# Split-weight tiles 64 bytes longer each, so that their offsets modulo 512 all differ

## The chip, the cores and the metric

The kernel runs on one core of a Trainium2 chip. The metric is the device time of one execution in microseconds (us), the median of three runs. A profile of one more execution gives the busy times of the engines: TensorE with its matmuls (PE) and its weight loads (PEld), VectorE (DVE), ScalarE (ACT), GpSimd (POOL) and the queue of SyncE (SP).

## What is computed

Two transformer blocks, one after the other, over 256 tokens of width 2048, in float32. The first mixes a gated linear attention and a sparse attention and ends with a feed-forward layer of width 5632; the second is an attention layer with modulation and a pooling layer. Cut to what matters here, it is a chain of matrix products with large weights:

```
proj = rms_norm(x, g) @ w_in                       # 2048 x 5672
h    = x + concat([gla_out, nsa_out]) @ w_out
x    = h + (silu(m @ w_gate) * (m @ w_up)) @ w_down   # 5632 wide
...
proj = h @ ev_w_in;   x = x + gate * _rmsnorm(y @ ev_w_out, post_g)
proj = h @ od_w_in;   x = x + gate * _rmsnorm(y @ od_w_out, post_g)
```

## The kernel before

**A product in three passes.** Every large product is made of float32r matmuls. Both sides are split into a high part and a remainder (hi = the value cast to float32r, lo = value - hi), and hi*hi, lo*hi and hi*lo are added up in PSUM. A job (class Job) is one panel of 512 weight columns. It goes through its K dimension in chunks of two tiles of 128 rows (per = 2), and `run` handles the chunks of all jobs in one list. For chunk i it issues the load of the weights of chunk i+4 into a tile `raw` (line 293, SP queue), splits those of chunk i+2 in `cut` (line 314: ACT casts raw to whi; line 315: DVE subtracts, raw - whi to wlo), and issues the matmuls of chunk i in `part`. raw has 6 buffers in the pool wp; whi and wlo have 3 each in wp. In two short stretches of the second block (the end of each output product) every other group of three chunks takes its whi and wlo from a pool of its own, "lead".

**Plain and turned jobs.** In a plain job the weights move: TensorE loads 128 columns of an activation tile (xh or xl) as the stationary operand, and 512 columns of whi or wlo stream through (lines 360 to 362; a chunk has 2 token halves x 2 tiles of K x 3 = 12 matmuls). In a turned job the activations move: 128 columns of whi or wlo are the stationary operand, and the 256 tokens of xh or xl stream through (lines 350 to 352; 4 x 2 x 3 = 24 matmuls per chunk). Every matmul loads its own stationary operand first.

**Where the activations lie.** The pairs xh, xl ([128, 16, 256] float32r, 16,384 bytes per partition each) are in actA for the first projection, the gate and up products, the context, and both output products of the second block; in actB for the first output product, two of the three down products, and the inputs of the second block's two layers; in the pool ffn for one down product. The inputs of the four small products of the pooling layer, ph and pl, lie in the pool pl2. Plain jobs with actA as the stationary operand have 3,744 matmuls, with actB 2,016, with ffn 384. Turned jobs with actA as the moving operand have 768 (the first projection), with actB 1,536, with ph/pl 192.

**Offsets in a partition.** Pools on the left are stacked in the order cp, xp, wp, actA, sp, actB, modp, lead; those on the right (ffn, pl2 and the pools of the attentions among them) grow down from the top, 229,376. Each tile's size is rounded up to 32 bytes. Adding this up gives, in bytes:

| tiles | start | modulo 512 |
|---|---|---|
| raw, 6 of 4,096 | 40,288 | 352 (o) |
| whi, 3 of 4,096 | 64,864 | o |
| wlo, 3 of 4,096 | 77,152 | o |
| actA: xh, xl | 89,440 and 105,824 | o |
| sp (scratch, 14,528 in all) | 122,208 | |
| actB: xh, xl | 136,736 and 153,120 | 32 (o + 192) |
| lead: whi, wlo | 181,088 | o |
| ffn: xh, xl; pl2: ph, pl | 196,576 and 212,960; 208,864 and 212,960 | 480 (o + 128) |
| the raw tiles of `compress`; its split tiles | 139,680; 157,856 | 416; 160 |

The small products in the attentions have tiles at other offsets: the first attention's values at 160, the second's keys and values at 416. `gla` uses gsumt and lah at 160. The table's last row belongs to line 900, which subtracts as line 315 does.

**The two scratch tiles.** `small(n, tag, bufs)` takes a tile from sp, which stays open to the end. `post_small` (the gates, line 705) uses ge, 48 floats, and `compress` (line 932) uses hs, 64 floats; each has one buffer and is used once.

Of the kernel before, what the change touches and what calls it, by code (L numbers as in the profile page):

```python
# [11 lines left out]
F32 = mybir.dt.float32  # L12
F32R = mybir.dt.float32r
# [6 lines left out]
P = 128  # L20
# [105 lines left out]
def emit(ctx, tc, a, out, dbg=None, stop=None):  # L126
# [8 lines left out]
    def pool(name, side, **kw):  # L135
        return tc.tile_pool(name=name, bufs=1, side=side, **kw)
# [3 lines left out]
    wp = ctx.enter_context(pool("wp", "left"))  # L140
# [6 lines left out]
    def nm(s):  # L147
        cnt[0] += 1
        return f"{s}_{cnt[0]}"
# [12 lines left out]
    def small(n, tag="sm", bufs=4):  # L162
        return sp.tile([P, n], F32, tag=f"{tag}{n}", name=nm(tag), bufs=bufs)
# [14 lines left out]
    def split(src, hi, lo, scale=None):  # L178

        if scale is None:  # L180
            S.copy(hi, src)  # L181
            V.tensor_tensor(lo, src, hi, OP.subtract)  # L182
        else:
            S.activation(hi, src, AF.Copy, scale=scale)
            V.scalar_tensor_tensor(lo, src, scale, hi.bitcast(F32), OP.mult, OP.subtract)
# [55 lines left out]
    def wait(*jobs):  # L241
        while not all(j.task and j.task.done for j in jobs):
            yield
# [22 lines left out]
                    mods.popleft()  # L266

    LOAD, SPLIT = 4, 2
    raws, splits = {}, {}

    def raw_tile():
# [2 lines left out]
    def run(jobs):  # L274
# [22 lines left out]
        def cut(i, eng=V):  # L297
            if i >= len(seq) or i in splits:
                return
            j, c = seq[i]  # L300
            nk, n = len(j.chunks[c]), j.n
            raw = raws.pop(i)
            wpool, bufs = (env["lead"], 3) if env.get("lead") and (i - env["lead0"]) % 6 >= 3 else (wp, 3)
            hi = wpool.tile([P, 2, 512], F32R, tag="whi", name=nm("whi"), bufs=bufs)
            lo = wpool.tile([P, 2, 512], F32R, tag="wlo", name=nm("wlo"), bufs=bufs)
            if j.per != 2:
                hi, lo = (t.rearrange("p k n -> p (k n)")[:, :nk * n].rearrange("p (k n) -> p k n", n=n) for t in (hi, lo))
            splits[i] = (hi, lo)
            if i == 0:
                for k in range(2):  # L310
                    x_split(0, (k,))()
                    split(raw[:, k, :], hi[:, k, :], lo[:, k, :])
                return
            S.copy(hi[:, :nk, :n], raw[:, :nk, :n])  # L314
            eng.tensor_tensor(lo[:, :nk, :n], raw[:, :nk, :n], hi[:, :nk, :n], OP.subtract)  # L315
# [152 lines left out]
    env = {}  # L468
# [77 lines left out]
    def x_split(c, ks=(0, 1)):  # L546
        def f():
            for j in ks:
                k = 2 * c + j
                split(xts[c][:, j, :], nx[0][:, k, :], nx[1][:, k, :], attn_g[:, k:k + 1])  # L550
        return f
# [139 lines left out]
    def post_small(ps):  # L691

        lrT, la, gates = env["lrT"], env["la"], env["gates"]
        V.memset(lrT, 1.0)
        V.tensor_tensor(lrT[:40, :], ps[0][:40, :T], Rrow[:40, :], OP.mult)
        yield
        yield from wait(jk1)
        pt = bank("t")[:, :80].rearrange("p (m n) -> p m n", m=2)
        zs = [bank(t) for t in "os"]
        for m in range(2):  # L700
            TE.transpose(pt[:, m, :], lrT[:40, tok(m)], ident[:40, :40])
        for m in range(2):
            TE.matmul(zs[m], lrT[:, tok(m)], env["w2aug"], start=True, stop=True)
        yield
        ge = small(48, "ge", 1).rearrange("p (m n) -> p m n", m=2)
        S.activation(ge, pt[:, :, 16:], AF.Exp, scale=-1.0)
        az = [tk() for _ in range(2)]
        for m in range(2):
            S.activation(az[m], zs[m], AF.Abs)
            V.tensor_scalar(la[:, m, :], zs[m], 0.0, None, OP.min)  # L710
        V.tensor_scalar(ge, ge, 1.0, None, OP.add)
        V.reciprocal(gates, ge)
        yield
        for m in range(2):
            S.activation(az[m], az[m], AF.Exp, scale=-1.0)
        yield
        for m in range(2):
            S.activation(az[m], az[m], AF.Ln, bias=ones)
        yield
        for m in range(2):  # L720
            V.tensor_tensor(la[:, m, :], la[:, m, :], az[m], OP.subtract)
# [157 lines left out]
    def compress():  # L879

        kgs = env["kgs"]
        env["es_cmp"] = ExitStack()
        cpp = env["cpp"] = env["es_cmp"].enter_context(pool("cmp", "right"))
        raws_, cuts_ = {}, {}
        seq = [(kv, c) for kv in range(2) for c in range(4)]

        def w1_load(i):
            if i < 8:
                kv, c = seq[i]
                t = raws_[i] = cpp.tile([P, 2, 4, P], F32, tag="w1", name=nm("w1"), bufs=2)  # L890
                for h in range(2):
                    r0 = (16 * h + 4 * c) * P
                    Y.dma_start(t[:, h], a[("cmp_k_w1", "cmp_v_w1")[kv]][r0:r0 + 4 * P, :].rearrange("(o d) j -> d o j", d=P))

        def w1_cut(i):
            if i < 8:
                t = raws_.pop(i)
                hi, lo = cuts_[i] = [cpp.tile([P, 2, 4, P], F32R, tag=f"w1{n}", name=nm("w1"), bufs=b) for n, b in (("h", 2), ("l", 1))]
                S.copy(hi, t)
                V.tensor_tensor(lo, t, hi, OP.subtract)  # L900

        w1_load(0)
        w1_load(1)
        w2t = cpp.tile([P, 2, P], F32, name="w2t")
        for kv in range(2):
            G.dma_start(w2t[:, kv, :], a[("cmp_k_w2", "cmp_v_w2")[kv]])
        csel = cpp.tile([68, 60], F32, name="cselt")
        G.dma_start(csel, a["csel"])
        yield
        w1_cut(0)  # L910
        yield from wait(jkcvc)
        U = env["U"]
        hp = bank("o")
        for i, (kv, c) in enumerate(seq):
            hi, lo = cuts_.pop(i)
            o = hp[:, kv * 256:(kv + 1) * 256]
            w1_load(i + 2)
            for j in range(4):
                first = c + j == 0
                TE.matmul(o[:68], U[kv][:, 4 * c + j, :], hi[:, :, j, :], start=first, stop=False, skip_group_check=True)  # L920
            for j in range(4):
                TE.matmul(o[:34], U[kv][:, 4 * c + j, :34], lo[:, :, j, :], start=False, stop=c + j == 6, skip_group_check=True)
            w1_cut(i + 1)
            yield
        seg = cpp.tile([P, 2, 4, P], F32, tag="w1", name=nm("seg"), bufs=2)[:68, :, :2, :]
        S.copy(seg, hp[:68, :].rearrange("p (v a j) -> p v a j", v=2, a=2))
        yield
        hp = bank("o")
        for kv in range(2):
            for k in range(2):  # L930
                TE.matmul(hp[:, 32 * kv:32 * kv + 30], seg[:, kv, k, :], csel[:, 30 * k:30 * k + 30], start=k == 0, stop=k == 1)
        hs = small(64, "hs", 1)
        for kv in range(2):
            S.activation(hs[:, 32 * kv:32 * kv + 30], hp[:, 32 * kv:32 * kv + 30], AF.Silu)
        yield
        op_ = bank("o")
        for kv in range(2):
            for h in range(2):
                c0 = 32 * kv + h * NCMP
                TE.matmul(op_[:NCMP, (2 * kv + h) * P:(2 * kv + h + 1) * P], hs[:, c0:c0 + NCMP], w2t[:, kv, :],  # L940
                          start=True, stop=True)
        yield
        V.tensor_copy(env["vcN"], op_[:NCMP, 256:512].rearrange("p (h d) -> p h d", d=P))
        kc = cpp.tile([P, 2, 4, P], F32, tag="w1", name=nm("kc"), bufs=2)[:, 0, :2, :]
        ss = small(2, "kcs")
        for h in range(2):
            S.activation(kc[:NCMP, h, :], op_[:NCMP, h * P:(h + 1) * P], AF.Square, accum_out=ss[:NCMP, h:h + 1])
        rr = rsqrt_mean(ss[:NCMP], 2, P, "kcr", NCMP)
        yield
        for h in range(2):  # L950
            V.tensor_scalar(kc[:NCMP, h, :], op_[:NCMP, h * P:(h + 1) * P], rr[:NCMP, h:h + 1], None, OP.mult)
        yield
        pt = bank("o")
        for h in range(2):
            TE.transpose(pt[:, h * 16:h * 16 + NCMP], kc[:NCMP, h, :], ident[:NCMP, :NCMP])
        yield
        V.tensor_scalar(env["kcT"], pt[:, :32].rearrange("p (h n) -> p h n", n=16)[:, :, :NCMP], kgs[:, 0:1], None, OP.mult)
        dump("kcT", env["kcT"])
        dump("vcN", env["vcN"])
        env["es_cmp"].close()  # L960
# [986 lines left out]
```

## Time and profile before

| | |
|---|---|
| median of 3 runs | 1950.67 us (1948.8 to 1950.82) |
| the profiled execution | 1954.03 us |
| its span, first to last instruction | 1952.3 us |
| PE busy | 1904.4 us, 98% |
| PEld busy | 1623.0 us, 83% |
| DVE busy | 1422.0 us, 73% |
| ACT busy | 956.8 us, 49% |
| DMA | 443.17 MB, mean 227 GB/s |

Busy times are those of one execution. Matmuls are pipelined: a matmul's record lasts longer than the distance to the start of the next, so the rate is read from the starts.

### The profile page before, as it was taken

How to read it: one execution, taken by the hardware profiler on the slowest of the kernel's cores; microseconds unless marked ns; L12 is line 12 of the kernel's file. 1: busy time of each engine (PE TensorE's matmuls, PEld its weight loads, DVE VectorE, ACT ScalarE, POOL GpSimd, SP SyncE). 2: the span in 40 equal slices, each digit the busy share in tenths (PEclk: the TensorE clock that was granted, in tenths of full speed). 3: DMA queues.
4: the chain of work that ended last, by engine and by line, in shares of the span. 5: the costliest groups of instructions: out<-in, count | busy, mean ns of one | idle time of the engine just before them, and what ended most of it. 6: DMA issues, size and time to landing. Idle time of an engine off the chain costs nothing.

```text
span 1952.3 us, 26733 instructions
## 1 busy us (share of the span) xinstructions
PE 1904.4 (98%) x10070; PEld 1623.0 (83%) x10070; DVE 1422.0 (73%) x1915; ACT 956.8 (49%) x1353; POOL 143.7 (7%) x142
## 2 busy tenths in 40 slices
PE   8999999999999999999999999999999998999998
PEld 8898778888888888888888787877999976999986
DVE  5767987688887888876667776569887777765554
ACT  6655456665444444444445444345556545544443
POOL 1001420000000000000000000012111003200001
PEclk9999999999999999999999999999999999999999
DMA  8675343478888888778987886465666695776544
GB/s 301 183 245 152 109 131 107 168 241 270 263 266 268 261 270 264 264 270 284 334 285 248 307 309 204 145 215 179 191 198 195 243 334 188 249 230 183 181 173 172
DMA packets 212434, 443.17 MB, mean 227 GB/s; under 512 B 18466, under 2 KB 27728, under 8 KB 211664
## 3 DMA queue, kind: packets, MB, share of 16 engines
q1 hardware_dynamic: 211536, 439.41, 68.2%
q0 software_dynamic: 768, 2.05, 0.3%
q8 instruction: 79, 1.29, 0.3%
q14 instruction: 51, 0.42, 0.1%
HBM read 439.29 MB, written 2.11 MB: 226 GB/s over the span
## 4 chain that ended last, share of the span: by engine, by line
PE 83%; DVE 5%; DMA 4%; ACT 4%; POOL 2%; issue 1%; SPq 0%; DVEq 0%; ACTq 0%; POOLq 0%
PE g L362 21%; PE g L360 21%; PE g L361 20%; PE g L350 5%; PE g L352 5%; PE g L351 5%; DVE wlo L315 1%; DMA raw<-in_w_down_dram 1%; ACT whi L314 1%; PE s L196 1%; DMA raw<-in_w_gate_dram 1%; PE o L1555 1%; PE t L196 1%; DMA raw<-in_od_mod_w_dram 1%; POOL E L757 1%
## 5 line engine op out<-in xcount | busy, mean ns | idle before, releaser
L315 DVE TENSOR_TENSOR wlo<-raw,whi 128x1024 fp32r<-128x1024 f32 x592 | 725.9, 1230 | 379.2 <-ACT whi L314 375.8
L314 ACT CAST whi<-raw 128x1024 fp32r<-128x1024 f32 x600 | 628.8, 1050 | 699.0 <-PE g L361 511.8
L360 PE MATMUL g<-whi,xh 128*128 128x512 f32 x2048 | 809.2, 395 | 3.5 <-ACT xh L1357 2.1
L362 PE MATMUL g<-wlo,xh 128*128 128x512 f32 x2048 | 802.4, 392 | 5.5 <-DVE wlo L315 5.5
L361 PE MATMUL g<-whi,xl 128*128 128x512 f32 x2048 | 801.4, 391 | 2.2 <-DVE xl L1362 2.2
L362 PEld LDWEIGHTS g<-wlo,xh 128*128 128x128 f32 x2048 | 385.5, 188 | 92.6 <-DVE wlo L315 9.5
L360 PEld LDWEIGHTS g<-whi,xh 128*128 128x128 f32 x2048 | 385.9, 188 | 85.5 <-ACT xh L1357 3.8
L361 PEld LDWEIGHTS g<-whi,xl 128*128 128x128 f32 x2048 | 385.8, 188 | 84.8 <-DVE xl L1362 4.8
L512 DVE SCALAR_TENSOR_TENSOR raw<-raw,crow 128x1024 f32<-128x1024 f32 x192 | 235.5, 1227 | 18.1 <-DMA raw<-in_od_mod_w_dram 8.8
L350 PE MATMUL g<-xh,whi 128*128 128x256 f32 (+1 forms) x784 | 222.3, 284 | 3.2 <-ACT whi L314 2.6
L352 PE MATMUL g<-xh,wlo 128*128 128x256 f32 (+1 forms) x784 | 220.3, 281 | 0.9 <-DVE wlo L315 0.5
L351 PE MATMUL g<-xl,whi 128*128 128x256 f32 (+1 forms) x784 | 220.0, 281 | 0.0
L350 PEld LDWEIGHTS g<-xh,whi 128*128 128x128 f32 (+1 forms) x784 | 148.1, 189 | 5.1 <-ACT whi L314 2.8
L352 PEld LDWEIGHTS g<-xh,wlo 128*128 128x128 f32 (+1 forms) x784 | 148.3, 189 | 1.7 <-DVE wlo L182 0.9
L351 PEld LDWEIGHTS g<-xl,whi 128*128 128x128 f32 (+1 forms) x784 | 148.3, 189 | 0.5
L512 DVE SCALAR_TENSOR_TENSOR mjk<-raw,crow 128x1024 bf16<-128x1024 f32 x64 | 78.0, 1218 | 2.6 <-ACT crow L501 2.0
L1537 POOL TENSOR_TENSOR P<-P,rc 128x512 f32<-128x512 f32 x32 | 34.2, 1069 | 161.5 <-DVE rc L1536 139.9
L189 POOL TENSOR_SCALAR crt<-rss 128x2 f32<-128x2 f32 x1 | 1.1, 1092 | 495.2 <-DVE rss L1280 495.2
L1529 ACT ACTIVATE P<-s,ngm 128x512 f32<-128x512 f32 x32 | 22.1, 690 | 26.5 <-DVE ngm L1522 13.8
L189 POOL TENSOR_SCALAR rrt<-rs 128x2 f32<-128x2 f32 x2 | 1.3, 642 | 405.2 <-DVE rs L1175 405.2
L196 PE MATMUL s<-ident,P 128*128 128x128 f32 x176 | 26.8, 275 | 1.0 <-DVE ngm L1519 0.6
L181 ACT CAST xh<-s 128x512 fp32r<-128x512 f32 x27 | 15.9, 588 | 22.2 <-PE s L196 22.2
(356 smaller groups left out, 1481.5 us busy)
## 6 DMA issues: line engine op xcount, KB each, us to landing
raw<-in_ev_mod_w_dram SPq DMA_DIRECT2D x96, 512.0 KB, 4.7
raw<-in_od_mod_w_dram SPq DMA_DIRECT2D x96, 512.0 KB, 4.9
raw<-in_w_gate_dram SPq DMA_DIRECT2D x88, 512.0 KB, 4.6
raw<-in_w_up_dram SPq DMA_DIRECT2D x88, 512.0 KB, 4.6
raw<-in_w_down_dram SPq DMA_DIRECT2D x88, 512.0 KB, 5.3
raw<-in_w_in_dram SPq DMA_DIRECT2D x87, 512.0 KB, 3.7
raw<-in_ev_w_in_dram SPq DMA_DIRECT2D x80, 512.0 KB, 4.4
raw<-in_od_w_in_dram SPq DMA_DIRECT2D x64, 512.0 KB, 4.5
```

The source lines that it names most:

```text
L196: TE.transpose(pt[:, j * P:(j + 1) * P], src[:, j * P:(j + 1) * P], ident)
L314: S.copy(hi[:, :nk, :n], raw[:, :nk, :n])
L315: eng.tensor_tensor(lo[:, :nk, :n], raw[:, :nk, :n], hi[:, :nk, :n], OP.subtract)
L350: TE.matmul(o, hi[:, k, ws], xh[:, xk, :], **b, stop=False, skip_group_check=True)
L351: TE.matmul(o, hi[:, k, ws], xl[:, xk, :], start=False, stop=False, skip_group_check=True)
L352: TE.matmul(o, lo[:, k, ws], xh[:, xk, :], start=False, **e, skip_group_check=True)
L360: TE.matmul(o, xh[:, xk, tok(m)], hi[:, k, :j.n], **b, stop=False)
L361: TE.matmul(o, xl[:, xk, tok(m)], hi[:, k, :j.n], start=False, stop=False)
L362: TE.matmul(o, xh[:, xk, tok(m)], lo[:, k, :j.n], start=False, **e)
L512: V.scalar_tensor_tensor(to, rv, 1.0, crow[:, s if both else h, :], OP.mult, OP.mult, accum_out=acc[:, slots.index(slot), h, t:t + 1])
L1529: S.activation(Pt, st[u]["sb"], AF.Exp, bias=ngm, accum_out=sm[m][:, g:g + 1])
L1537: G.tensor_tensor(Pt, Pt, rc.to_broadcast([P, 512]), OP.mult)
```

## The change

Each of the six tiles of split weights in wp is allocated 1,040 floats long in place of 1,024, and the first 1,024 are used as before, through the same [128, 2, 512] view. The tiles of the pool lead keep their length. `ge` becomes a tile of the pool gla, which ends with the gated linear attention, and `hs` one of the pool cmp, which ends with `compress`; both leave sp.

```diff
     LOAD, SPLIT = 4, 2
+    WT = 1024 + 16
...
-            hi = wpool.tile([P, 2, 512], F32R, tag="whi", name=nm("whi"), bufs=bufs)
-            lo = wpool.tile([P, 2, 512], F32R, tag="wlo", name=nm("wlo"), bufs=bufs)
+            hi, lo = (wpool.tile([P, WT if wpool is wp else 1024], F32R, tag=t, name=nm(t), bufs=bufs)[:, :1024].rearrange("p (k n) -> p k n", k=2)
+                      for t in ("whi", "wlo"))
...
-        ge = small(48, "ge", 1).rearrange("p (m n) -> p m n", m=2)
+        ge = env["glp"].tile([P, 48], F32, name="ge").rearrange("p (m n) -> p m n", m=2)
...
-        hs = small(64, "hs", 1)
+        hs = cpp.tile([P, 64], F32, name="hs")
```

## Rows read from the trace of the kernel before

**Rows 1.** The page, part 1 (busy us, share of the span, instructions of each engine) and part 4 (the chain of work that ended last, share of the span by engine).
```profile
PE 1904.4 (98%) x10070; PEld 1623.0 (83%) x10070; DVE 1422.0 (73%) x1915; ACT 956.8 (49%) x1353; POOL 143.7 (7%) x142
...
PE 83%; DVE 5%; DMA 4%; ACT 4%; POOL 2%; issue 1%; SPq 0%; DVEq 0%; ACTq 0%; POOLq 0%
```

**Rows 2.** Groups of instructions by line with different shapes kept apart, over the whole span: line, engine, operation, out<-in, shapes, count | busy us, mean ns of one | idle time of the engine before them, and what ended it.
```profile
L360 PE MATMUL g<-whi,xh 128*128 128x512 f32 x2048 | 809.2, 395 | 3.5 <-ACT xh L1357 2.1 <-ACT whi L314 1.1
L362 PE MATMUL g<-wlo,xh 128*128 128x512 f32 x2048 | 802.4, 392 | 5.5 <-DVE wlo L315 5.5
L361 PE MATMUL g<-whi,xl 128*128 128x512 f32 x2048 | 801.4, 391 | 2.2 <-DVE xl L1362 2.2
L315 DVE TENSOR_TENSOR wlo<-raw,whi 128x1024 fp32r<-128x1024 f32 x591 | 725.1, 1231 | 377.8 <-ACT whi L314 374.5 <-PE o L940 1.4
L314 ACT CAST whi<-raw 128x1024 fp32r<-128x1024 f32 x599 | 628.0, 1050 | 697.9 <-PE g L361 511.8 <-PE g L351 80.7 <-DMA raw<-in_w_down_dram 28.9
...
L350 PE MATMUL g<-xh,whi 128*128 128x256 f32 x768 | 217.9, 284 | 3.2 <-ACT whi L314 2.6 <-ACT whi L181 0.6
...
L350 PE MATMUL g<-ph,whi 128*128 128x256 f32 x64 | 18.0, 282 | 0.0
...
L900 DVE TENSOR_TENSOR w<-w,w 128x1024 fp32r<-128x1024 f32 x8 | 9.8, 1223 | 7.0 <-ACT w L899 4.3 <-PE o L922 1.8 <-ACT whi L314 0.9
```

**Rows 3.** Busy time of each engine in the six stretches of rows 4 to 9: window, its length, busy us and count of PE, PEld, DVE, ACT and POOL, granted clock of TensorE (1.00 is 2.4 GHz), busy share of the DMA engines, GB/s.
```profile
589.70:611.00 21.30, 21.30 (x95) 17.65 (x94) 16.21 (x21) 9.69 (x10) 0.00 (x0) 1.00 0.82 268
835.60:857.10 21.50, 21.50 (x96) 17.64 (x95) 16.06 (x23) 7.91 (x9) 0.00 (x0) 1.00 0.83 294
1031.60:1053.00 21.40, 21.40 (x93) 17.34 (x92) 15.57 (x23) 10.38 (x13) 0.00 (x0) 1.00 0.63 216
29.60:41.00 11.40, 11.40 (x98) 11.40 (x97) 4.46 (x8) 7.23 (x14) 0.00 (x0) 1.00 0.85 285
1684.60:1695.00 10.40, 10.40 (x94) 10.40 (x93) 7.85 (x11) 4.81 (x5) 0.10 (x1) 1.00 0.90 300
1798.30:1803.90 5.60, 5.60 (x49) 5.60 (x48) 3.21 (x4) 2.59 (x3) 2.05 (x2) 1.00 0.53 148
```

**Rows 4.** Timeline in a gate/up product (plain, actA): start us, us, engine, line, operation, out<-in. The first and the last matmul of 94 in a row from 590 to 611 us, and between them some rows with the weight loads at 600 us.
```profile
589.71 0.39 PE L362 MATMUL g<-wlo,xh 128*128 128x512 f32 x1
...
599.91 0.39 PE L362 MATMUL g<-wlo,xh 128*128 128x512 f32 x1
599.91 0.19 PEld L360 LDWEIGHTS g<-whi,xh 128*128 128x128 f32 x1
600.14 0.39 PE L360 MATMUL g<-whi,xh 128*128 128x512 f32 x1
...
610.79 0.39 PE L362 MATMUL g<-wlo,xh 128*128 128x512 f32 x1
```

**Rows 5.** The same in the first down product (plain, actB): the first and the last of 94 matmuls from 836 to 857 us, and between them some rows of all engines at 845 to 848 us.
```profile
835.69 0.39 PE L361 MATMUL g<-whi,xl 128*128 128x512 f32 x1
...
845.73 1.05 ACT L314 CAST whi<-raw 128x1024 fp32r<-128x1024 f32 x1 [1.70 <-PE g L361]
845.76 0.39 PE L360 MATMUL g<-whi,xh 128*128 128x512 f32 x1
...
846.45 0.40 PE L360 MATMUL g<-whi,xh 128*128 128x512 f32 x1
...
847.13 0.39 PE L360 MATMUL g<-whi,xh 128*128 128x512 f32 x1
...
847.82 0.39 PE L360 MATMUL g<-whi,xh 128*128 128x512 f32 x1
...
856.98 0.39 PE L361 MATMUL g<-whi,xl 128*128 128x512 f32 x1
```

**Rows 6.** The same in the second down product (plain, ffn): the first and the last of 92 matmuls from 1032 to 1053 us.
```profile
1031.64 0.40 PE L360 MATMUL g<-whi,xh 128*128 128x512 f32 x1
...
1052.78 0.41 PE L361 MATMUL g<-whi,xl 128*128 128x512 f32 x1
```

**Rows 7.** The same in the first projection (turned, actA): the first and the last of 94 matmuls from 29.9 to 40.9 us.
```profile
29.68 0.28 PE L350 MATMUL g<-xh,whi 128*128 128x256 f32 x1
...
40.84 0.28 PE L350 MATMUL g<-xh,whi 128*128 128x256 f32 x1
```

**Rows 8.** The same in the gate of the pooling layer (turned, actB): the first and the last of 91 matmuls from 1685 to 1695 us.
```profile
1684.73 0.28 PE L352 MATMUL g<-xh,wlo 128*128 128x256 f32 x1
...
1694.93 0.28 PE L352 MATMUL g<-xh,wlo 128*128 128x256 f32 x1
```

**Rows 9.** The same in a small product of the pooling layer (turned, ph/pl): the last matmul before it and its last one, with 48 intervals between them.
```profile
1798.09 0.28 PE L352 MATMUL g<-xh,wlo 128*128 128x256 f32 x1
...
1803.79 0.28 PE L352 MATMUL g<-ph,wlo 128*128 128x256 f32 x1
```

**Rows 10.** Timeline of all engines at two places in the attentions of the first block where a plain matmul with wlo is followed by one whose stationary operand lies at 160 (lah, line 749, and nvh, line 1100).
```profile
228.44 0.39 PE L362 MATMUL g<-wlo,xh 128*128 128x512 f32 x1
...
228.66 0.63 PE L749 MATMUL s<-gsumt,lah 128*128 128x512 f32 x2
...
301.86 0.39 PE L362 MATMUL g<-wlo,xh 128*128 128x512 f32 x1
...
302.08 0.40 PE L1100 MATMUL o<-pT,nvh 128*128 128x256 f32 x2
```

## The prediction

> **What bounds the kernel now.** I read the page first: TensorE is busy 98% of the span and carries 83% of the chain that ended last [rows 1]. DVE (73%) and ACT are behind it, so what counts is how close together the matmuls start. The groups by line show where these are: 6,144 products with a moving operand 512 wide (lines 360 to 362, "plain") and 2,496 that are 256 wide (lines 350 to 352, "turned"), with next to no idle time in front of them [rows 2]. A matmul's busy time (395 ns) is no price, since the next one starts long before it ends. The price is the distance between starts, and that I took from the timeline of TensorE in six stretches where it never waits, at a granted clock of 1.00, the level of 2.4 GHz [rows 3]. With (last start - first start) / intervals:
>
> - plain, stationary in actA (whi/wlo and actA at the same offset modulo 512): 21.08 us / 93 = 226.7 ns [rows 4]
> - plain, stationary in actB: 21.29 / 93 = 228.9 ns [rows 5]
> - plain, stationary in the ffn pool: 21.14 / 91 = 232.3 ns [rows 6]
> - turned, moving in actA: 11.16 / 93 = 120.0 ns [rows 7]
> - turned, moving in actB: 10.20 / 90 = 113.3 ns [rows 8]
> - turned, moving in ph/pl: 5.70 / 48 = 118.8 ns [rows 9]
>
> Same code, same shapes, same clock, and yet 226.7 to 232.3 and 113.3 to 120.0. The offsets differ. The timeline also shows that the weights of the next matmul begin to load in the same 10 ns as the running matmul [rows 4]: two reads of SBUF run side by side. So I take d = (offset of the next weights - offset of the moving tile) modulo 512 as what sorts the stretches. From the offsets in the section on the kernel: 0, 192, 128 for the plain ones and 0, 320, 384 for the turned ones. Steps of 512 and 1024 bytes within xh (the loops over k and m) don't change the spacing, so the period is no longer than 512. ACT and DVE do not matter here: in actB three matmuls take 0.69 us (845.76 to 846.45) while the cast of line 314 runs and 0.69 us (847.13 to 847.82) after it [rows 5]. Two single plain products whose next weights stand at d = 320 (wlo, then nvh or lah) take 0.22 us [rows 10]: no more than at d = 0.
>
> So 226.7 and 113.3 ns look like the floor of the two shapes, and the excess over it is what the offsets cost: plain 0 (d = 0), 0 (320), 2.3 (192), 5.6 (128); turned 6.7 (d = 0), 0 (320), 5.4 (384).
>
> **The change, part by part.** *The longer tiles.* 1,040 floats make 4,160 bytes, so that with raw's offset as o the three whi stand at o, +64, +128, the three wlo at +192, +256, +320. All behind them moves too: actA goes to +384 (6 x 64). No instruction is added, none is wider: the slices still take 1,024 elements. *The two scratch tiles.* ge (192 bytes) and hs (256) leave sp, so all behind them on the left falls by 448 - 384 = 64 bytes: actB goes from o+192 to o+128; the pools on the right (ffn, ph) stay at o+128. Neither is on a path by itself: each is written and read within one task, and no queue gets an instruction or a wait more: 0 us. The cover of that is that compress and post_small are over before their pools' space is taken again; if a later tile waited for it, it would be once, and all the waits of a group of TensorE together are 5.5 us at most [rows 2].
>
> *The splits themselves.* Line 315 reads raw and whi and writes wlo, all three at one offset now: 1231 ns; line 900 does the same with tiles at two offsets (the raw ones 256 bytes apart from the split ones), 1223 ns [rows 2]. At most 8 ns per instruction are in it, on an engine that is off the path: 0.
>
> *The distances.* Now d differs by buffer. Each chunk (12 plain or 24 turned products) uses one pair, two of three intervals in the case of whi, the third with wlo. (In plain code the first two intervals have whi moving; in turned code two of three have whi next.)
>
> - plain, actA: whi 384, 320, 256; wlo 192, 128, 64
> - plain, actB and ffn: whi 128, 64, 0; wlo 448, 384, 320
> - turned, actA: whi 128, 192, 256; wlo 320, 384, 448
> - turned, actB and ph: whi 384, 448, 0; wlo 64, 128, 192
>
> Where a row shows the distance for the shape I take it. The others are bounded by 0 and the largest excess of the shape (5.6, 6.7); nothing below the floor shows up in any stretch, so none may gain on it. In between I take the mean of those shown: plain (0+0+2.3+5.6)/4 = 2.0, turned (6.7+0+5.4)/3 = 4.0. Counts follow from the jobs (16 tiles of k, 2 or 4 tiles of the other side, 3 products).
>
> - plain actA, 3,744: whi (2.0+0+2.0)/3 = 1.3, wlo (2.3+5.6+2.0)/3 = 3.3; mean (2 x 1.3 + 3.3)/3 = 2.0, before 0: +7.4 us [rows 4, 5, 6, 10]
> - plain actB, 2,016: whi (5.6+2.0+0)/3 = 2.5, wlo 1.3; 2.1, before 2.3: -0.4 us [rows 5]
> - plain ffn, 384: 2.1, before 5.6: -1.3 us [rows 6]
> - turned actA, 768: whi 4.0, wlo (0+5.4+4.0)/3 = 3.1; 3.7, before 6.7: -2.3 us [rows 7, 9]
> - turned actB, 1,536: whi (5.4+4.0+6.7)/3 = 5.4, wlo 4.0; 4.9, before 0: +7.5 us [rows 8]
> - turned ph, 192: 4.9, before 5.4: -0.1 us [rows 9]
>
> Sum +10.8 us. TensorE is busy for 1904.4 of 1952.3 us [rows 1]; where it waits, slower matmuls hide, so 97.5% of it counts: +10.5 us. With all unknown distances at 0 the same table gives +3.3 - 2.1 - 1.7 - 4.7 + 4.1 - 0.5 = -1.6 us, with all at their largest +15.0 + 2.9 - 0.7 - 0.7 + 9.9 + 0.2 = +26.6 us. The profiled execution would go from 1954.0 to 1964.5 us; the median of the runs shown is 3.4 us below that execution, and on it the forecast is 1950.7 + 10.5 = 1961.2 us.
>
> The reading that carries this is a plain one: most of the kernel's matmuls (3,744) stand at the one distance that costs nothing, and any other can only be as good. Why equal offsets are free for 512 columns and dear for 256 the stretches show only in outline: in the turned ones the weight load is busy all the time (11.40 of 11.40 us), in the plain ones 83% of it [rows 3], so that loading 128 columns takes about as long as streaming 256, and the moving read would run about twice as fast through the addresses (an inference). With d = 0 a matmul of 512 starts level and draws ahead; with d = 64 to 256 it catches up with the load once. A matmul of 256 lasts no longer than the load, so that any stop of the load is seen.
>
> **The rivals.** (1) *The distances do nothing, or even out.* Against: 113.3 beside 120.0 ns at one clock [rows 3, 7, 8]. For: each of the groups moves from one known value to a mixture, and the signs differ (+7.4, -2.3, +7.5). Time: 1950.7. The Trainium skill ("TensorE: Matmul & The Clock Gate", "Step-by-step: what each phase is for") says that TensorE has two independent read ports and that loading the next weights takes no bandwidth from the running matmul; by it the change would be worth 0. By that rule the six stretches would be two values, and they are six.
>
> (2) *Faster: changing the distance every chunk keeps the collision from settling, and all groups go to the floor.* Each steady excess goes: 768 x 6.7 + 2,016 x 2.3 + 384 x 5.6 + 192 x 5.4 = 5.1 + 4.6 + 2.2 + 1.0 = 12.9 us, times 97.5%: 1938.1. It wins when d = 384, 256 and 64 cost under about 0.5 ns each for plain products and the turned ones in actB lose nothing. Against: d = 128 and 192 occur for wlo in actA and cost 5.6 and 2.3 now.
>
> (3) *The floor is none.* 512 columns at 2.4 GHz are 213.3 ns; if 226.7 is itself a collision of equal offsets, 13.3 ns x 6,144 = 82 us could go: 1869. Against: d = 320 gives 0.22 us [rows 10], and no stretch has a spacing below the 226.7 [rows 4 to 6]. The Trainium skill (same page, "Wait — 56ns, not 53.3ns?") gives 215.7 ns for 512 columns back to back, which would be 11 ns below this; no run here shows it.
>
> (4) *Far slower: each new pair restarts the collision, so all go to the largest excess.* 3,744 x 5.6 + 2,016 x 3.3 + 1,536 x 6.7 + 192 x 1.3 = 21.0 + 6.7 + 10.3 + 0.2 = 38.2 us, times 97.5%: 1988.
>
> **How the numbers follow.** About 0.2% (3.9 us) is what a measurement of this kernel can tell from no change. Forecast 0.59, of which 0.06 lies within 3.9 us; (1) 0.16; (2) 0.10; (3) 0.03; (4) 0.12. So faster 0.13, same 0.16 + 0.06 = 0.22, slower 0.53 + 0.12 = 0.65. The range takes in the bounds of the sum (1949.1 to 1976.6), (1), and the nearer part of (2): 1946 to 1977.
>
> **What the profile after would show.** Right: starts 228 to 230 ns apart where the stationary operand is in actA (lines 360 to 362, for instance in the 22 gate and up products), no longer in an even beat but in one that changes with the buffer; turned products in actB at 116 to 120, those of the first projections below 120; lines 314 and 315 within 1% of 1050 and 1231 ns; TensorE's idle time and the DMA as before. Wrong: 226.7 kept in actA with mixed distances (then the forecast loses its largest term), turned products in actB still at 113.3, or a spacing below 226.

## The result, and the profile after

Before 1950.57 us (median of 4 runs, 1948.80 to 1950.82), after 1964.66 us (4 runs, 1962.92 to 1967.53): 0.72% slower, ratio 1.0072, 95% interval 1.0060 to 1.0084, and 3.5 us from the forecast of 1961.2. The profiled execution of after took 1966.4 us (span 1964.6); before's took 1954.0. In after every line behind the diff's first hunk stands one lower: 361 to 363 are the plain products, 351 to 353 the turned ones, 315 and 316 the two halves of the split.

The page of after, part 1 and part 4 (columns as in rows 1):

```profile
PE 1922.1 (98%) x10070; PEld 1627.9 (83%) x10070; DVE 1422.1 (72%) x1915; ACT 956.3 (49%) x1353; POOL 145.4 (7%) x142
...
PE 82%; DMA 6%; DVE 5%; ACT 3%; issue 2%; POOL 2%; SPq 1%; DVEq 0%; ACTq 0%; POOLq 0%
```

The instructions are the same in number, and DVE and ACT are as busy as before [rows 1]; TensorE has gained 17.7 us of busy time. Groups of instructions by line of after, different shapes apart (columns as in rows 2):

```profile
L361 PE MATMUL g<-whi,xh 128*128 128x512 f32 x2048 | 812.0, 397 | 1.7 <-ACT xh L1358 1.3 <-ACT whi L315 0.2
L363 PE MATMUL g<-wlo,xh 128*128 128x512 f32 x2048 | 808.7, 395 | 3.5 <-DVE wlo L316 3.4
L362 PE MATMUL g<-whi,xl 128*128 128x512 f32 x2048 | 805.2, 393 | 0.5 <-DVE xl L1363 0.4
L316 DVE TENSOR_TENSOR wlo<-raw,whi 128x1024 fp32r<-128x1024 f32 x591 | 725.2, 1231 | 385.6 <-ACT whi L315 382.1 <-PE o L941 1.3
L315 ACT CAST whi<-raw 128x1024 fp32r<-128x1024 f32 x599 | 626.8, 1048 | 708.6 <-PE g L362 513.3 <-PE g L352 80.6 <-DMA raw<-in_w_down_dram 30.2
```

The subtract is at 1231 ns and the cast at 1048, beside 1231 and 1050 in rows 2: the spread of the six tiles does not slow the engines that write them. The idle time in front of the three plain lines fell from 3.5 + 5.5 + 2.2 = 11.2 us to 1.7 + 3.5 + 0.5 = 5.7; part of that is the single execution (two kernels below whose plain products follow each other about as closely as before's have 10.1 and 8.0). Timeline of TensorE in after: first and last matmul of the stretches of rows 4 to 8, the same instructions each (93, 93, 91, 93 and 90 intervals, granted clock 1.00 in all five):

```profile
591.65 0.40 PE L363 MATMUL g<-wlo,xh 128*128 128x512 f32 x1
...
613.07 0.39 PE L363 MATMUL g<-wlo,xh 128*128 128x512 f32 x1
...
841.23 0.39 PE L362 MATMUL g<-whi,xl 128*128 128x512 f32 x1
...
862.66 0.39 PE L362 MATMUL g<-whi,xl 128*128 128x512 f32 x1
...
1039.61 0.39 PE L361 MATMUL g<-whi,xh 128*128 128x512 f32 x1
...
1060.57 0.39 PE L362 MATMUL g<-whi,xl 128*128 128x512 f32 x1
...
29.04 0.28 PE L351 MATMUL g<-xh,whi 128*128 128x256 f32 x1
...
39.99 0.28 PE L351 MATMUL g<-xh,whi 128*128 128x256 f32 x1
...
1693.04 0.28 PE L353 MATMUL g<-xh,wlo 128*128 128x256 f32 x1
...
1703.62 0.28 PE L353 MATMUL g<-xh,wlo 128*128 128x256 f32 x1
```

(Last start - first start) / intervals: plain 230.3, 230.4 and 230.3 ns, where before had 226.7, 228.9 and 232.3 [rows 4 to 6]; turned 117.7 and 117.6, where before had 120.0 and 113.3 [rows 7, 8]. What strikes is that the three plain stretches agree, although actA and actB now lie 256 bytes apart modulo 512.

Within a stretch the beat changes with the buffer. The first matmul of four chunks (12 products each) in the gate and up products:

```profile
592.58 0.39 PE L361 MATMUL g<-whi,xh 128*128 128x512 f32 x1
...
595.33 0.40 PE L361 MATMUL g<-whi,xh 128*128 128x512 f32 x1
...
598.09 0.39 PE L361 MATMUL g<-whi,xh 128*128 128x512 f32 x1
...
600.87 0.39 PE L361 MATMUL g<-whi,xh 128*128 128x512 f32 x1
```

From the starts in ns the three chunks are at 229.4, 229.7 and 232.0 ns a product, and this goes on in threes, as there are three buffers; in before the chunks of this stage that hold no wait are at 226.7 to 227.0.

The intervals from each matmul's start to the next one's, added up over one profiled execution of each kernel by group (spacing: mean of those that hold no wait, counted as those under 258 ns plain and under 152 ns turned):

| group | forecast, us | measured, us | spacing before, ns | after |
|---|---|---|---|---|
| plain, actA | +7.4 | +8.6 | 227.2 | 230.5 |
| plain, actB | -0.4 | +4.4 | 229.2 | 230.5 |
| plain, ffn | -1.3 | -1.7 | 232.5 | 230.6 |
| turned, actA | -2.3 | -1.7 | 119.6 | 117.6 |
| turned, actB | +7.5 | +4.4 | 114.5 | 117.4 |
| turned, ph | -0.1 | -0.1 | 118.7 | 118.3 |
| all other matmuls | 0 | -1.7 | | |
| sum | +10.8 | +12.3 | | |

12.3 us lie between the two profiled executions; before's is 3.4 us above its median and after's 1.7 above its own, so the medians are 14.1 apart. The sums hold the waits of these two executions; the spacings do not.

### The profile page after: what moved, and what is told of

It reads as the page before. It is cut to its first block, busy times and chain, and to the rows that moved or that the text cites. A ratio compares the mean times of both kernels' runs of the same rounds, so it can differ in the third digit from the quotient of the medians.

```text
span 1964.6 us, 26733 instructions
## 1 busy us (share of the span) xinstructions
PE 1922.1 (98%) x10070; PEld 1627.9 (83%) x10070; DVE 1422.1 (72%) x1915; ACT 956.3 (49%) x1353; POOL 145.4 (7%) x142
## 4 chain that ended last, share of the span: by engine, by line
PE 82%; DMA 6%; DVE 5%; ACT 3%; issue 2%; POOL 2%; SPq 1%; DVEq 0%; ACTq 0%; POOLq 0%
PE g L363 20%; PE g L362 20%; PE g L361 20%; PE g L351 5%; PE g L352 5%; PE g L353 5%; DMA raw<-in_od_mod_w_dram 3%; DMA raw<-in_w_down_dram 1%; DVE wlo L316 1%; PE s L196 1%; ACT whi L315 1%; PE o L1556 1%; PE t L196 1%; POOL E L758 1%; DVE xres L1662 0%
## 5 line engine op out<-in xcount | busy, mean ns | idle before, releaser
L315 ACT CAST whi<-raw 128x1024 fp32r<-128x1024 f32 x600 | 627.6, 1048 | 709.6 <-PE g L362 513.3
```

## The experiments

Three theories stood. A: what counts is the distance d of the prediction (start of the next weights - start of the moving tile) modulo 256. B: the same modulo 512, as the prediction had it. C: what counts is something else in the change, as the six tiles' differing among themselves.

**Moving the activations, with the six tiles left at one offset.** Three kernels, with n = 96, 64 and 16 floats (384, 256 and 64 bytes):

```diff
+    actA.tile([P, n], F32, name="pad")
     nx = act_pair(actA)
...
-        ge = small(48, "ge", 1).rearrange("p (m n) -> p m n", m=2)
+        ge = env["glp"].tile([P, 48], F32, name="ge").rearrange("p (m n) -> p m n", m=2)
...
-        hs = small(64, "hs", 1)
+        hs = cpp.tile([P, 64], F32, name="hs")
```

> The kernel before, with the two scratch tiles moved as in the change and one unused tile of 384 bytes a partition at the head of the activations' pool. Both activation blocks then lie where the change puts them, but the six split tiles stay as long as they were and keep one offset modulo 512 among them. Distances: plain over the first block 384 (was 0), plain over the second block 128 (was 192), turned over the first block 128, turned over the second block 384 (was 320). Theory A, what counts is the distance of weights and moving tile modulo 256: plain over the first block rises from 226.7 to the 232.3 ns of the feed-forward products at 128, 3,744 x 5.6 = +21 us less what waits give back; plain over the second block 228.9 to 232.3, +7; turned over the second block 113.3 to 118.8, +8; turned over the first block 120.0 to 118.8, -1; sum +35, 1975 to 1987 us. Theory B, modulo 512 as in the prediction: the last two and the second block's plain products the same, the first block's at an untried distance, 0 to 5.6 ns more: 1965 to 1987 us. Theory C, what counts is that the six tiles differ among themselves (or that the scratch tiles moved): no change, 1949 to 1953 us.

> As the run with 384 bytes, with 256 bytes instead. Distances: plain over the first block 256 (was 0), plain over the second 0 (was 192), turned over the first 256 (was 0), turned over the second 0 (was 320). Theory A, modulo 256: plain over the first block stays at 226.7 ns, plain over the second falls from 228.9 to 226.7 (2,016 x 2.2 = -4 us), turned over the first stays at 120.0, turned over the second rises from 113.3 to 120.0 (1,536 x 6.7 = +10 us): 1955 to 1958 us. Theory B, modulo 512: the first block's two distances are untried; where 256 is any other than 0, plain over the first block is above 226.7 ns, or turned over the first below 120.0. Theory C, the spread of the six tiles among themselves: no change, 1949 to 1953 us.

> As the run with 384 bytes, with 64 bytes instead. Distances: plain over the first block 64 (was 0), plain over the second 320 (was 192), turned over the first 448 (was 0), turned over the second 192 (was 320). Theory A, modulo 256: plain at 64 is plain at 320, as single products of before had it, so both plain groups sit at 226.7 ns (second block -4 us); turned at 448 and at 192 are one distance, which the six buffers of the changed kernel, taken as distances modulo 256, put at about 116.8 ns: first block 768 x -3.2 = -2.5 us, second 1,536 x 3.5 = +5.4 us; sum -1, 1947 to 1952 us. Theory B, modulo 512: the turned groups need not agree with each other, and plain over the first block may lie anywhere from 226.7 to 232.3 ns, up to +21 us. Theory C, the spread of the six tiles: no change, 1949 to 1953 us.

Measured: 384 bytes 1977.07 us, ratio 1.0132 (1.0111 to 1.0152); 256 bytes 1955.29 us, 1.0021 (1.0011 to 1.0031); 64 bytes 1979.81 us, 1.0137 (1.0115 to 1.0159); before beside them 1951.33. Timelines of TensorE, the instructions of rows 4, 5 and 8 (93, 93 and 90 intervals), first with 384 bytes:

```profile
595.06 0.40 PE L362 MATMUL g<-wlo,xh 128*128 128x512 f32 x1
...
616.68 0.40 PE L362 MATMUL g<-wlo,xh 128*128 128x512 f32 x1
...
1700.31 0.28 PE L352 MATMUL g<-xh,wlo 128*128 128x256 f32 x1
...
1710.99 0.28 PE L352 MATMUL g<-xh,wlo 128*128 128x256 f32 x1
```

with 256 bytes:

```profile
588.36 0.39 PE L362 MATMUL g<-wlo,xh 128*128 128x512 f32 x1
...
609.43 0.39 PE L362 MATMUL g<-wlo,xh 128*128 128x512 f32 x1
...
834.06 0.39 PE L361 MATMUL g<-whi,xl 128*128 128x512 f32 x1
...
855.14 0.39 PE L361 MATMUL g<-whi,xl 128*128 128x512 f32 x1
...
1680.69 0.28 PE L352 MATMUL g<-xh,wlo 128*128 128x256 f32 x1
...
1691.49 0.28 PE L352 MATMUL g<-xh,wlo 128*128 128x256 f32 x1
```

and with 64 bytes:

```profile
594.60 0.40 PE L362 MATMUL g<-wlo,xh 128*128 128x512 f32 x1
...
616.30 0.39 PE L362 MATMUL g<-wlo,xh 128*128 128x512 f32 x1
...
847.26 0.40 PE L361 MATMUL g<-whi,xl 128*128 128x512 f32 x1
...
868.97 0.39 PE L361 MATMUL g<-whi,xl 128*128 128x512 f32 x1
```

With 384 bytes, gate and up go to 21.62 / 93 = 232.5 ns, the price that the feed-forward products have at 128 [rows 6], and the turned products in actB to 118.7. The six tiles are equal here and the loss is larger than that of the change, so C is out. With 256 bytes gate and up stay at 226.6 (distance 256, was 0), the first down product falls to 226.7 (distance 0, was 192), and the turned products in actB rise to 120.0 (distance 0): 256 is as 0, which is A. With 64 bytes A's time (1947 to 1952 us) was a miss: the two plain stretches stand at 233.3 and 233.4 ns, distances 64 and 320. That they agree is A; the price that I had taken for 320, from two single products [rows 10], was wrong. The turned groups, at distances 448 and 192, come to 117.7 and 117.0 ns over the whole execution (116.8 had been expected of both).

**The disputed cost by itself**, one moving tile mv and one weights tile st, 20 distances (the two loops are functions in the kernel):

```
for d in STEPS:                      # 0, 32, ... 480, 4, 16, 48, 240
    w = st[:, d // 4:d // 4 + P]
    for _ in range(48): TE.matmul(acc, w, mv[:, :512], start=True, stop=True)
    for _ in range(48): TE.matmul(acc[:, :256], w, mv[:, :256], start=True, stop=True)
```

> Only the disputed cost, none of the layers: 60 products to warm up, then for each of 20 distances d of the weights from the moving tile (0, 32, ... 480, and 4, 16, 48, 240 bytes) 48 products 512 wide and 48 products 256 wide, weights loaded anew for each, while VectorE and ScalarE do nothing; the output is filled with a copy of the last product. Theory A, modulo 256: the 512-wide spacing is 226.7 ns at 0 and 256, 232.3 at 128 and 384, about 228.9 at 192 and 448; the 256-wide is 120.0 at 0 and 256, 113.3 at 64 and 320, 118.8 at 128 and 384; the second half of the distances repeats the first. Theory B, modulo 512: the same numbers at 0, 128, 192 and 0, 320, 384, but the halves differ. Theory C, the other engines' or the six tiles' traffic is the cause: one spacing at all distances.

Part 1 of its page (columns as in rows 1), and from its timeline the first matmul of a group of 48 wide ones (line 32) and of the 48 narrow ones behind it (line 36), at distances 0, 64, 256 and 320:

```profile
PE 352.7 (96%) x1980; PEld 307.2 (84%) x1980; DVE 0.7 (0%) x1; ACT 3.3 (1%) x3; POOL 0.2 (0%) x4
```

```profile
22.64 0.39 PE L32 MATMUL acc<-mv,st 128*128 128x512 f32 x1
...
33.52 0.28 PE L36 MATMUL acc<-mv,st 128*128 128x256 f32 x1
...
56.15 0.40 PE L32 MATMUL acc<-mv,st 128*128 128x512 f32 x1
...
67.35 0.28 PE L36 MATMUL acc<-mv,st 128*128 128x256 f32 x1
...
157.07 0.40 PE L32 MATMUL acc<-mv,st 128*128 128x512 f32 x1
...
167.97 0.28 PE L36 MATMUL acc<-mv,st 128*128 128x256 f32 x1
...
190.60 0.40 PE L32 MATMUL acc<-mv,st 128*128 128x512 f32 x1
...
201.80 0.28 PE L36 MATMUL acc<-mv,st 128*128 128x256 f32 x1
```

Over 48 products: (33.52 - 22.64) / 48 = 226.7 ns at 0 and (67.35 - 56.15) / 48 = 233.3 at 64; the second half repeats it, 10.90 / 48 = 227.1 at 256 and 233.3 at 320. Without the first six intervals of each group the means are:

| distance, and distance + 256 | 0 | 32 | 64 | 96 | 128 | 160 | 192 | 224 |
|---|---|---|---|---|---|---|---|---|
| 512 wide, ns | 226.7 | 233.4 | 233.3 | 234.2 | 232.4 | 233.2 | 228.9 | 233.3 |
| 256 wide, ns | 120.0 | 118.3 | 113.3 | 118.6 | 119.9 | 120.1 | 117.8 | 116.7 |

The two halves differ by less than 0.05 ns in every column. TensorE alone, with DVE and ACT at rest, gives the numbers of the layers: A. What counts lies between the weight load and the moving stream of TensorE itself; by which means, these runs do not show. The Trainium skill ("TensorE: Matmul & The Clock Gate", "Step-by-step: what each phase is for") has the two on independent read ports, so that the load takes no read bandwidth from the running matmul. Here the place of the next weights alone moves the spacing of the same matmul from 226.7 to 234.2 ns.

**Finer, and with both tiles moved.** The same kernel with steps of 4 bytes, and with four other starts of the moving tile:

> Only the disputed cost again, none of the layers; the output is filled with a copy of the last product. First the distances 0 to 252 bytes in steps of 4, 30 products 512 wide and 30 products 256 wide at each; then the moving tile's start is moved by 32, 64, 128 and 192 bytes and the weights with it, at distances 0, 64, 128 and 192. Theory A, only the distance counts, modulo 256: whatever the moving tile's start, 226.7, 233.3, 232.4 and 228.9 ns at 512 wide and 120.0, 113.3, 119.9 and 117.8 ns at 256 wide. Rival, the place of the weights or of the moving tile by itself counts: the four starts differ from one another at one distance. The fine steps have no expectation of theory A but that neighbours of 0 are slower at 512 wide (232 to 233 ns at 4, 16 and 48 in the coarse run) and that 240 is again at 226.7.

At 512 columns the start does not count: at all four, 226.7 to 227.1, 233.3, 232.1 and 228.9 ns. At 256 columns it does not at distances 0, 64 and 192 (120.0, 113.3 and 117.8); at 128 the four moved starts agree at 118.5 to 118.8, but the first has 120.0. Of the 64 distances none is below 226.7 wide or 113.3 narrow; 226.7 is there at 0, 100, 120, 132, 204 and 252, and the highest is 243.3 at 156. At 240, where the 226.7 of the coarse run was expected again, 228.3 was measured: the distance alone does not settle the spacing to 2 ns.

**The order of the kernel.** One moving tile at one distance is not what a chunk does. Four tiles in the kernel's order (slices left out):

```
for _ in range(24):
    TE.matmul(acc, xh, hi, start=True, stop=False)
    TE.matmul(acc, xl, hi, start=False, stop=False)
    TE.matmul(acc, xh, lo, start=False, stop=True)
```

> Only products, none of the layers, now in the order of the kernel's: high part of the activations with high part of the weights, low with high, high with low, from four tiles whose starts are set one by one; 24 such triples 512 wide and 24 turned ones 256 wide for each set of starts; the output is filled with a copy of the last product. Sets (xh, xl, hi, lo): four with equal pairs at 0, 64, 128 and 192 from the weights; the three states of the changed kernel's buffers modulo 256, (128, 128, 0, 192), (128, 128, 64, 0) and (128, 128, 128, 64); and the mixed view of the run before, (0, 192, 0, 0). Reading one, each product has the price of its own distance: equal pairs give 226.7, 233.3, 232.4, 228.9 ns plain; the changed kernel's three states give (2 x 232.4 + 228.9)/3 = 231.2, (2 x 233.3 + 232.4)/3 = 233.0 and (2 x 226.7 + 233.3)/3 = 228.9, mean 231.0; the mixed view gives (2 x 226.7 + 228.9)/3 = 227.4. Reading two, a product's price hangs also on its neighbours: the three states have the 230.5 of the changed kernel as their mean, and the mixed view 231.1, as it measured in the run before.

Timeline: first plain matmul (line 32) and first turned one (line 38) of the three states of the changed kernel, and of a "mixed view" (xh at distance 0 and xl at 192, as in the next kernel); 72 intervals between the two of each pair:

```profile
123.55 0.39 PE L32 MATMUL acc<-hi,xh 128*128 128x512 f32 x1
...
140.26 0.28 PE L38 MATMUL acc<-xh,hi 128*128 128x256 f32 x1
...
148.81 0.39 PE L32 MATMUL acc<-hi,xh 128*128 128x512 f32 x1
...
165.45 0.28 PE L38 MATMUL acc<-xh,hi 128*128 128x256 f32 x1
...
173.79 0.40 PE L32 MATMUL acc<-hi,xh 128*128 128x512 f32 x1
...
190.29 0.28 PE L38 MATMUL acc<-xh,hi 128*128 128x256 f32 x1
...
198.77 0.39 PE L32 MATMUL acc<-hi,xh 128*128 128x512 f32 x1
...
215.41 0.28 PE L38 MATMUL acc<-xh,hi 128*128 128x256 f32 x1
```

16.71, 16.64 and 16.50 us over 72 are 232.1, 231.1 and 229.2 ns, mean 230.8 (without the first nine of each, 232.2, 231.1 and 228.9, mean 230.7): the 230.3 to 230.6 of the changed kernel. Turned, the three come to 118.7, 115.6 and 117.8, mean 117.3: its 117.4 to 117.7. The first two states are not what reading one gives (231.2 and 233.0), and the mixed view stands at 231.1, dearer than either of its distances (226.7 and 228.9). Reading two holds for the means. State by state it is not settled: the chunks of the changed kernel are at 232.0, 229.4 and 229.7, and the three states here at 232.2, 231.1 and 228.9.

**Two kernels for the distances that were found good** (the first ran before the run of triples):

```diff
+    def act_pair(p, at=(0, 16), more=(48, 16)):
+        return tuple(p.tile([P, KT * T + e], F32R, tag=t, name=nm(t), bufs=1)[:, s:s + KT * T].rearrange("p (k t) -> p k t", k=KT)
+                     for t, e, s in zip(("xh", "xl"), more, at))
...
+    nx = act_pair(actA, (48, 0))
...
```

> The kernel before with six split tiles at one offset, the two scratch tiles moved, and activation tiles up to 192 bytes longer, in which each stage takes a view at the distance that the runs of products alone found good modulo 256: 0 for plain products, 64 for turned ones. The first activations (read turned 768 times at 120.0 ns and plain 672 times) go from 0 to 64 turned and to 192 plain; of the second block's plain products two thirds of those whose activations are never read turned go from 192 to 0; the feed-forward products go from 128 to 0. Theory A, distance modulo 256: turned over the first block 768 x (120.0 - 113.3) = -5.1 us, feed-forward 384 x (232.4 - 226.7) = -2.2 us, the plain ones moved in both directions 704 and 672 and cancel; sum -7.3 us less what waits take back: 1942 to 1946 us. Rival, the kernel's end is set elsewhere and waits take all of it: 1949 to 1952 us.

Measured 1950.67 us beside 1950.71, ratio 1.0000 (0.9990 to 1.0009): the time of the rival, though waits explain only a part of it, since the spacings by themselves gave 1.5 us and not 7.3. Its groups, as in the table of the result: feed-forward 232.5 to 227.6 ns, yet the sum of its 384 intervals 93.6 us before and after (92.3 to 93.9 in the four kernels here that left this stage alone). What PE waited for in that stage (1026.6 to 1121 us; total, times, longest), in the kernel before:

```profile
PE g L362 <- DVE wlo L315: 1.6, 3, 0.5
PE g L360 <- ACT whi L314: 1.0, 1, 1.0
```

and in this one (lines one higher):

```profile
PE g L361 <- DVE wlo L314: 2.5, 6, 0.5
PE g L359 <- ACT whi L313: 1.1, 1, 1.1
```

Products that come sooner wait longer for their weights: three more waits, 1.0 us, of the 360 x 4.9 ns = 1.8 us gained. This is one execution of each; the four kernels that left the stage alone have two or three waits in it, 1.6 to 1.9 us. Turned products over the first block fell to 116.1 ns only, and their sum by 1.2 us. The mixed views lost 2.2 us (1,056 products; 231.1 ns in the first down product, 228.9 before).

The second gives both halves of an activation one distance, only where it is never read turned:

```diff
+        env["mix"] = act_pair(env["actB"], (0, 16), (48, 16))
...
+        env["hx"] = act_pair(env["actB"], (48, 0), (48, 16))
...
```

> The kernel before with the six split tiles at one offset and the two scratch tiles moved; tiles of the second block are 192 and 64 bytes longer, and the 1,056 plain products whose activations there are never read turned take both their halves at distance 0 (were at 192), so that no mixed triple arises; the activations read turned as well stay at 192 plain and 64 turned. Reading two (a triple with one distance has the price of that distance): 1,056 x (228.9 - 226.7) = -2.3 us, of which half or all is left: 1948.3 to 1949.6 beside 1950.7. Reading one expects the same; it had also expected a gain of the mixed view and is told apart by the run of triples. Rival, waits take the gain as they did at the feed-forward products: no difference.

Measured 1949.45 beside 1950.37 us, ratio 0.9995 (0.9986 to 1.0004): 0.9 us faster, where half to all of 2.3 us had been expected, and within what can be told from no change: neither a gain nor its absence is shown by the time. The instructions of rows 5 (93 intervals) take 21.08 us in its timeline, 226.7 ns, and took 228.9: there theory A is borne out.

**All kernels together.** For each group, the change of its spacing times its number of intervals without a wait; the sum of the six groups, beside the difference of the medians:

| kernel | by spacing, us | by medians, us |
|---|---|---|
| the change | +16.8 | +14.1 |
| 384 bytes | +31.4 | +25.7 |
| 64 bytes | +31.9 | +28.5 |
| 256 bytes | +4.8 | +4.0 |
| first of the two good distances | -1.5 | 0.0 |
| second | -2.4 | -0.9 |

So the spacings account for most of each time, and in the three large losses 11% to 18% of it does not reach the end. The last two rows lie within the noise.

## Why the prediction was right, step by step

**The bound and the price: right.** The spacing of TensorE sorted by d = (next weights - moving tile) is what the runs of products alone show, without any other engine; the period is 256 and not 512.

**The splits and the scratch tiles at 0: right** (1231 and 1048 ns). The shifted kernels hold the moved scratch tiles too, and with 256 bytes the gate and up products are at 226.6 ns.

**The largest term, plain actA, +7.4: right in mechanism, measured +8.6.** Two errors met. The mean excess is 3.3 to 3.6 ns and not 2.0: d = 320 was put at 0 from two single products [rows 10], and a row of them costs 6.7 (233.3). The two were read rightly: of the 12 such products in before's trace 11 are at 225 or 226 ns. But a single one does not have the price of a row. Against it, more than 2.5% is hidden: 3,679 intervals without a wait x 3.3 ns = 12.1 us, and the sum rose by 8.6. That 3.5 us is too much, since before's profiled execution is 3.4 us above its median: with 256 bytes, where the spacing of this group is as before (227.3 beside 227.2), its sum fell by 2.6 us too. By the medians a sixth is hidden (14.1 of 16.8 us).

**Plain actB, -0.4: mis-sized, measured +4.4** (2.7 by its spacing). This is the same wrong 320, and a period that I had bounded from above only ("no longer than 512"). It is 256: actA's three buffers (384 and 192, 320 and 128, 256 and 64) and actB's (128 and 448, 64 and 384, 0 and 320) are then the same three states, and all plain groups had to end at one spacing. Ffn, from 5.6 above the floor to the same spacing, gained 1.7 (forecast 1.3), of which its spacing explains 0.7.

**Turned actB, +7.5: too large, measured +4.4.** Its unknown distances 448, 64, 128 and 192 were put at 4.0, and 0 and 384 at 6.7 and 5.4; the mixture stands at 117.4, 4.1 above the floor and not 4.9, and before's own mean was 114.5 and not 113.3, as part of these products stand at 117.8 (last section). That the two groups of actA and actB must meet (117.6 and 117.4) follows again from 256.

**A step that held by luck:** a price for each product by its own distance, averaged. The run of triples shows that neighbours count; in the changed kernel's three states the two readings give 231.0 and 230.7 ns. Luck is also in the closeness of the sum: by spacing plain actA and actB cost 4.7 and 3.1 us more than forecast and turned actB 3.1 less, and the waits that took back 2.7 us had been put at 0.3.

**The signs.** The beat that changes with the buffer came as said, turned products in actB at 117.6 and those of the first projection at 117.7 too; plain starts are at 230.3 to 230.4 where 228 to 230 had been said, and the idle time did not stay.

**The rivals.** (1) is out by the run with 384 bytes. (2) is out: the changing buffers don't bring the floor back. (3) found no support: of 64 distances none goes below 226.7 ns. The Trainium skill ("TensorE: Matmul & The Clock Gate", "Wait — 56ns, not 53.3ns?") has 215.7 ns for 512 columns; no run here shows it. (4) would have all plain products at 232.3 ns; they are at 230.5, and of the three states in the run of triples the one with whi at distance 0 is the cheapest, 228.9.

**Open:** why the spacing depends on the distance as it does. The 64 fine steps follow no order that I could find, and the prediction's inference, that the stream of 512 columns catches up with the load once at d = 64 to 256, does not fit: at 256 nothing is paid (226.6).

## What to carry to other kernels

Where matmuls follow each other without a wait, take their spacing from starts, stage by stage; if equal shapes at an equal clock differ, compare the offsets of stationary and moving tiles before anything else. Measure such a price in a row of the kernel's own order, not from a single instruction or a mean of others. And a slower spacing showed for the most part in the time (82% to 89% in the large losses here), while the feed-forward products, made faster, showed nothing in their sum: they waited longer for their weights.

## What was not expected of the hardware

- The spacing depends on the distance of two tiles modulo 256 bytes, from 226.7 to 243.3 ns for 512 columns and from 113.3 to 123.3 for 256, with TensorE alone (the repetition after 256 was tried at steps of 32 bytes).
- One distance can have two beats. In the kernel with the mixed views the turned products of the first block stand at distance 64, as those of the second block do at 113.3 ns [rows 8], and yet of the 22 chunks of 24 products without a gap 13 are at 117.6 to 117.9 ns and nine at 113.3 to 114.5. The kernel before has both beats at this distance too, in its turned products in actB: six chunks of 43 at 117.7 or 117.8. Timeline of the kernel with the mixed views, the instructions of rows 7: 10.95 / 93 = 117.7 ns. What chooses the beat was not tried.

```profile
29.40 0.28 PE L349 MATMUL g<-xh,whi 128*128 128x256 f32 x1
...
40.35 0.28 PE L349 MATMUL g<-xh,whi 128*128 128x256 f32 x1
```
